# A two-layer hybrid mixer kernel: GLA's steps moved ahead to S5's input, and an LRU block's second gate moved one piece back

## The chip, the cores and the metric

One core of a Trainium2 chip runs the whole program in one launch. The metric is the device time of that execution in microseconds (us), lower is better; what is shown is the median of several runs. A profiled execution gives the rows that are read below.

## The reference

The input is one sequence of 512 tokens of width 1024, in float32. Two layers follow each other; each normalises the stream, projects it, runs four causal mixers beside each other, multiplies each by its SiLU path, merges the four with sigmoid gates and adds the result to the stream. A final RMSNorm ends it.

```python
for l in range(DEPTH):                       # DEPTH = 2
    u = rmsnorm(h, norm_gain[l])
    (gq, gk, gv, glr, gg, rq, rk, rv, rg, lx, lg, su, sg) = split_columns(u @ w_in[l])
    o_gla = gla_mix(gq, gk, gv, glr, ...) * silu(gg)        # chunked linear attention, 8 chunks of 64
    o_ret = retention_mix(rq, rk, rv, ...) * silu(rg)
    o_lru = rglru_mix(lx, ...) * silu(lg)                   # conv of 4, two sigmoid gates, linear scan
    y5 = gelu(s5_scan(su, ...)); y5 = y5 * sigmoid(y5 @ s5_glu_w[l] + s5_glu_b[l])
    o_s5 = y5 * silu(sg)
    merged = sum(sigmoid(u @ w_merge_gate[l, b]) * (o_b @ w_branch[l, b]) for the four b)
    h = h + merged @ w_out[l]
return rmsnorm(h, final_norm_gain)
```

In `rglru_mix` the two gates are `r = sigmoid(xb @ w_a + b_a)` and `i = sigmoid(xb @ w_x + b_x)`; with `a = exp(-8 r softplus(-lam))` the scan is `h_t = a h_(t-1) + xc i sqrt(1 - a^2)`.

## The kernel before

**Projections.** Almost all of TensorE's time goes to products with streamed weights. Each weight tile of 128x1024 comes by one DMA (`emit_raw`, L234), is copied by ACT as `hi` (L242), and DVE forms the rest `lo` (L243); a product is then three matmuls, `hi·uh`, `hi·ul`, `lo·uh` (L268 to L270 in `mm3`). A projection `proj_c` makes 128 channels for 512 tokens: 8 parts, 24 matmuls of 128x512. `PLAN` sets the order of the projections; weights are made some projections ahead with high priority.

**Pieces.** After every second part of `mm3`, that is after six matmuls, `bg.tick()` is called; such a stretch is called a *piece*, and a projection has four. `Bg` (L176 and on) holds generators for background work. Each has a time in ticks, and at every tick the first one in the list whose time has come runs one step, at most one step a tick (`PER_TICK = 1`). What a generator yields is the number of ticks until its next step. TensorE's own order is the order in which the code is written out, tick by tick; for the other engines the framework's scheduler sets the order ahead of time, from the same program, and each engine then runs its list in order.

**PSUM.** The main products have three buffers (`PM = 3`, tag `pm`), and the LRU gates take theirs from the same three. Five buffers (`ps`) serve the small matmuls.

**The stretch that the change touches** lies in each layer between GLA's projections and the first merge. Four projections make S5's input (`proj_c()` in L894 to L897: ACT copies each into `su`, tag `c4a`, and 32 small DMAs bring it to `uc`). Eight projections follow for the LRU: for m = 0 to 3 one `lx` and one `lg`. After them `merge(0)` begins with two gate projections. Beside these run two kinds of generators:

- `gla_core` (L852 on): the first step transposes the keys (L861). Then `attention` (L647 on) runs for t = -1 to 4, one *step* each: `values` (L691), the transposes of the last step's output (L713), `inter` (L702), `scores` (L658), `kv` (L672), on DVE the masks (L866) and the state updates (L682), then `norm`: squares on ACT (L871), a sum on DVE (L873), a power on POOL (L287), the product on DVE (L877). The next step's transposes read that product.
- `lru_block` m (L904 on), added when `lx` of m is done. Its first step makes the convolution: L915 on ACT and three L917 on DVE read the `lx` buffer and write `xc`, whose buffer `ac0` or `ac4` is shared by blocks m and m+2. It then yields 9 ticks. The second step is gate 0 (three matmuls, L924) and its Tanh on ACT (L929). The third is gate 1 (L924 again), the ACT operations L934, L935, L936, the DVE operations L937 to L943, POOL's L942 and L945, the square root on ACT (L944, which needs another activation table, so a table load stands before it and one after it), and the scan L946 and L947 on DVE. L947 is the last reader of `xc`.

```python
pa = gate(0); tr = s2()
act.activation(tr, pa, AF.Tanh, scale=0.5, bias=hc[:, 3, m:m + 1])     # L929
yield 1
px = gate(1)
act.activation(gl, px, AF.Tanh, ...)                                   # L934
act.activation(tl, tr, AF.Tanh, ...); act.activation(rl, tr, AF.Exp, ...)   # L935, L936
```

Gates of block m stand inside the projection `lg` of m+1 (block 3's inside the second gate projection of the merge).

Of the kernel before, what the change touches and what calls it, by code (L numbers as in the profile page):

```python
# [104 lines left out]
def hybrid_kernel(tc, x, wch, wgv, pcols, wlr, lrubd, s5a, s5bc, s5d, gains, ident_d, smask_d, rmask_d, rope_d,  # L105
# [19 lines left out]
    def big(tag, shape, dt=F32):  # L125
        return bp.tile(shape, dt, tag=tag, name=nm(tag))

    def s2(shape=(P, 512), dt=F32):
        return sm.tile(list(shape), dt, tag="s2", name=nm("s2"), bufs=S2B)

    def one(tag, shape, dt=F32, bufs=1):
        return sm.tile(list(shape), dt, tag=tag, name=nm(tag), bufs=bufs)

    def tiny(shape):
        return sm.tile(list(shape), F32, tag="tiny", name=nm("ty"), bufs=12)

    def psm(shape=(P, 512)):
        return pm.tile(list(shape), F32, tag="pm", name=nm("pm"))

    def pss(shape=(P, 512)):  # L140
        return pp.tile(list(shape), F32, tag="ps", name=nm("ps"))
# [79 lines left out]
    bg = Bg()  # L221
# [52 lines left out]
    def split(dst_h, dst_l, src, scale=None):  # L274
        if scale is None:
            act.activation(dst_h, src, AF.Copy)
            dve.tensor_tensor(dst_l, src, dst_h.bitcast(F32), SUB)
        else:
            act.activation(dst_h, src, AF.Copy, scale=scale)
            dve.scalar_tensor_tensor(dst_l, src, scale, dst_h.bitcast(F32), op0=MUL, op1=SUB)  # L280


    def rstd_of(ss, n, scale):
        ms = tiny([P, n])
        dve.tensor_scalar(ms, ss, scale, EPS, op0=MUL, op1=ADD)  # L285
        r = tiny([P, n])
        pool.tensor_tensor(r, ms, neghalf[:, :n], ALU.pow)  # L287
        return r
# [497 lines left out]
    for l in range(DEPTH):  # L786
# [4 lines left out]
        v = big("v8", [P, NT, W])  # L791
# [15 lines left out]
        dec = one("dec", [P, 2, 8])  # L807
# [44 lines left out]
        S = big("S4", [P, 4, 2, DV])  # L852

        def gla_core(E=E, kt_=kt_, v=v, sil=sil, oh=oh, ol=ol, S=S, dec=dec, hc=hc):
            kt = one("kt", [P, NT, 256])
            for t2 in range(2):
                pt = pss([P, 2, 2, P])
                for j in range(2):
                    for hp in range(2):
                        tt = 2 * t2 + j  # L860
                        pe.transpose(pt[:, j, hp], kt_[:, hp, tt * P:(tt + 1) * P], ident)  # L861
                act.activation(kt[:, 2 * t2:2 * t2 + 2], pt.rearrange("p j a b -> p j (a b)"), AF.Copy)
            yield 3

            def mask(dst, src, par, r):
                dve.copy_predicated(dst, smask[r, None, :].to_broadcast([64, 2, 64]), src)  # L866

            def norm(po):
                sq = s2([P, 2, 2, DV])
                for par in range(2):  # L870
                    act.activation(sq[:, par], po[par], AF.Square)  # L871
                ss = tiny([P, 2, 2])
                dve.tensor_reduce(ss, sq, axis=AX.X, op=ADD)  # L873
                r = rstd_of(ss.rearrange("p a b -> p (a b)"), HEADS, 1.0 / DV).rearrange("p (a b) -> p a b", a=2)
                on = s2([P, 2, 2, DV])
                for par in range(2):
                    dve.tensor_tensor(on[:, par], po[par], r[:, par, :, None].to_broadcast([P, 2, DV]), MUL)  # L877
                return lambda h: on[:, h % 2, h // 2]

            def final(t, pT):  # L880
                ts = slice(t * P, (t + 1) * P)
                p = s2([P, HEADS, P])
                for h in range(HEADS):
                    dve.scalar_tensor_tensor(p[:, h], pT[:, h], hc[:, 0, h:h + 1], sil[:, h, ts], op0=MUL, op1=MUL)
                split(oh[:, :, ts], ol[:, :, ts], p)

            yield from attention(lambda b, hp, cs: E[b:b + 64, 0, hp, cs], lambda b, hp, cs: E[b:b + 64, 1, hp, cs],
                                 kt, v, S, lambda hp, n: dec[:, hp, n:n + 1], mask, norm, final, 6)

        gg_ = bg.add(gla_core(), 3)  # L890


        uc = [big(f"uc{i}", [P, 8, P]) for i in range(2)]
# [12 lines left out]
        def lru_block(m, ps, of):  # L906
            t0 = 4 * (m % 2)
            wbd = one("wbd", [P, 2, P])
            sp.dma_start(wbd, lrubd[l, :, m::4])
            wbh, wbl = one("wbh", [P, 2, P], F32R), one("wbl", [P, 2, P], F32R)  # L910
            split(wbh, wbl, wbd)
            xc = big(f"ac{t0}", [P, T])
            xh, xl = (big(f"ac{t0 + i}", [P, T], F32R) for i in (1, 2))
            cw = lambda j: pc[:, PC["cw"][0] + 4 * m + j:PC["cw"][0] + 4 * m + j + 1]
            act.activation(xc, ps, AF.Identity, scale=cw(3), bias=col("cb", m))  # L915
            for s in (1, 2, 3):
                dve.scalar_tensor_tensor(xc[:, s:], ps[:, :T - s], cw(3 - s), xc[:, s:], op0=MUL, op1=ADD)  # L917
            split(xh, xl, xc)
            yield 9

            def gate(i):
                g = psm()
                for n, (a, b) in enumerate(((wbh, xh), (wbh, xl), (wbl, xh))):
                    pe.matmul(g, a[:, i], b, start=n == 0, stop=n == 2)  # L924
                return g

            pa = gate(0)
            tr = s2()
            act.activation(tr, pa, AF.Tanh, scale=0.5, bias=hc[:, 3, m:m + 1])  # L929
            yield 1  # L930
            px = gate(1)
            gl = big(f"ac{t0 + 3}", [P, T])
            tl, rl = (big(f"ac{t0 + i}", [P, T]) for i in (1, 2))
            act.activation(gl, px, AF.Tanh, scale=0.5, bias=hc[:, 4, m:m + 1])  # L934
            act.activation(tl, tr, AF.Tanh, scale=spl[:, 0, m:m + 1], bias=spl[:, 0, m:m + 1])  # L935
            act.activation(rl, tr, AF.Exp, scale=spl[:, 2, m:m + 1], bias=spl[:, 2, m:m + 1])  # L936
            dve.tensor_scalar(rl, rl, 0.5, 0.5, op0=MUL, op1=ADD)  # L937
            q = s2()
            dve.scalar_tensor_tensor(q, tl, 1.0, rl, op0=ADD, op1=MUL)
            dve.scalar_tensor_tensor(rl, q, -2.0, rl, op0=ADD, op1=MUL)  # L940
            dve.scalar_tensor_tensor(gl, gl, 1.0, xc, op0=ADD, op1=MUL)
            pool.tensor_tensor(gl, gl, rl, MUL)  # L942
            dve.scalar_tensor_tensor(rl, tl, -1.0, rl, op0=ADD, op1=MUL)  # L943
            act.activation(tl, tl, AF.Sqrt)  # L944
            pool.tensor_tensor(gl, gl, tl, MUL)  # L945
            dve.tensor_tensor_scan(xc, rl, gl, 0.0, MUL, SUB)  # L946
            dve.scalar_tensor_tensor(of[:, m], xc, 0.5, of[:, m], op0=MUL, op1=MUL)  # L947

        lbs = []
        for m in range(4):  # L950
            ps = proj_c()
            if m >= 2:
                bg.finish(lbs[m - 2])
            lbs.append(bg.add(lru_block(m, ps, ofl)))
            silu2(ofl[:, m], proj_c())
# [293 lines left out]
```

## Time and profile before

| | |
|---|---|
| median of 3 runs | 1257.12 us (1256.19 to 1259.31) |
| the profiled execution | 1255.62 us |
| its span, first to last instruction | 1253.8 us |
| mean granted clock of TensorE | 0.996 of full speed |
| busy: PE, DVE, ACT, POOL | 1212.6, 809.8, 529.6, 508.4 us |
| PE in the 40 slices of the span | 9 tenths or more in 38, 5 in the first, 7 in the last |

A slice is 31 us. All rows of the trace are from that one profiled execution, so that sums are made against its 1255.62 us. A row of the timeline has the start, the duration, engine, line, operation, result and operands, and in brackets the idle time of the engine before it with what ended it. The duration of a matmul is modelled to its end in PSUM and is longer than its share of the engine: while TensorE is not held up, one 128x512 matmul starts about 0.23 us after the other.

### The profile page before, as it was taken

The page shows a single profiled execution, that of the slowest core. Times are in us where ns is not written, and L with a number is a line of the kernel's source. Part 1 is how long each engine was busy: PE and PEld are TensorE (multiplying, and loading weights), DVE is VectorE, ACT ScalarE, POOL GpSimd, SP SyncE. Part 2 cuts the span into 40 slices and gives each one's busy share as a digit, 9 for nine tenths or more (in the row PEclk, how much of TensorE's full clock was granted, in tenths as well). Part 3 has the DMA queues.
Part 4 walks back from the last instruction along what each step waited for, and adds up shares of the span by engine and source line. Part 5 has one row for each costly group of instructions (what it writes and reads, how often), then busy time and mean ns, then how long its engine had stood idle before and what let it go on. Part 6 is the DMA issues. An engine that isn't in the chain of part 4 may idle for free. (4 is left out here: it accounts for less than half of the span.)

```text
span 1253.8 us, 17315 instructions
## 1 busy us (share of the span) xinstructions
PE 1212.6 (97%) x6444; PEld 1008.0 (80%) x6444; DVE 809.8 (65%) x1411; ACT 529.6 (42%) x824; POOL 508.4 (41%) x588
## 2 busy tenths in 40 slices
PE   5999999989999999999999999999899999999997
PEld 5888868877888888888898887788778888888886
DVE  6974875477599896744354467746756988446433
ACT  5622475434434622532355235744345354333322
POOL 8780313578666568000201012238887563000001
PEclk9999999999999999999999999999999999999999
DMA  6233323213322423433342232232222234333322
GB/s 227 85 106 106 102 76 106 93 38 105 96 77 83 135 87 98 137 99 101 103 135 101 84 112 83 84 105 76 72 89 84 66 101 137 96 123 101 90 79 84
DMA packets 49796, 124.25 MB, mean 99 GB/s; under 512 B 8272, under 2 KB 21040, under 8 KB 49712
## 3 DMA queue, kind: packets, MB, share of 16 engines
q1 hardware_dynamic: 49712, 123.15, 31.2%
q8 instruction: 51, 0.84, 0.3%
q14 instruction: 33, 0.27, 0.1%
HBM read 114.73 MB, written 4.19 MB: 95 GB/s over the span
## 5 line engine op out<-in xcount | busy, mean ns | idle before, releaser
L243 DVE TENSOR_TENSOR lo<-raw,hi 128x1024 fp32r<-128x1024 f32 (+1 forms) x196 | 262.0, 1340 | 214.6 <-ACT hi L242 212.0
L268 PE MATMUL pm<-uh,hi 128*128 128x512 f32 x960 | 378.3, 394 | 5.0 <-ACT ac L934 3.3
L242 ACT ACTIVATE hi<-raw 128x1024 fp32r<-128x1024 f32 (+1 forms) x196 | 207.8, 1061 | 415.1 <-PE pm L269 284.6
L270 PE MATMUL pm<-uh,lo 128*128 128x512 f32 x960 | 374.4, 390 | 0.0
L269 PE MATMUL pm<-ul,hi 128*128 128x512 f32 x960 | 374.3, 390 | 0.0
L268 PEld LDWEIGHTS pm<-uh,hi 128*128 128x128 f32 x960 | 180.3, 188 | 48.7 <-ACT ac L934 5.0
L270 PEld LDWEIGHTS pm<-uh,lo 128*128 128x128 f32 x960 | 180.3, 188 | 37.9
L269 PEld LDWEIGHTS pm<-ul,hi 128*128 128x128 f32 x960 | 180.4, 188 | 36.2
L268 PE MATMUL pm<-oh,hi 128*128 128x512 f32 x256 | 101.0, 395 | 0.0
L270 PE MATMUL pm<-oh,lo 128*128 128x512 f32 x256 | 99.8, 390 | 0.0
L269 PE MATMUL pm<-ol,hi 128*128 128x512 f32 x256 | 99.8, 390 | 0.0
L1135 POOL TENSOR_TENSOR ac<-c4a,S 128x512 f32<-128x512 f32 x2 | 2.6, 1294 | 239.5 <-DVE c4a L1133 239.5
L287 POOL TENSOR_TENSOR ty<-ty,c 128x4 f32<-128x4 f32 x16 | 16.9, 1057 | 118.8 <-DVE ty L285 118.1
L358 PE MATMUL pm<-hi,uh 128*128 128x512 f32 x128 | 52.6, 411 | 5.1 <-ACT v L1028 3.8
L268 PEld LDWEIGHTS pm<-oh,hi 128*128 128x128 f32 x256 | 48.1, 188 | 11.3 <-issue 1.7
L270 PEld LDWEIGHTS pm<-oh,lo 128*128 128x128 f32 x256 | 48.1, 188 | 10.1
L269 PEld LDWEIGHTS pm<-ol,hi 128*128 128x128 f32 x256 | 48.1, 188 | 9.6
L360 PE MATMUL pm<-lo,uh 128*128 128x512 f32 x128 | 50.9, 398 | 0.0
L359 PE MATMUL pm<-hi,ul 128*128 128x512 f32 x128 | 50.9, 398 | 0.0
L531 POOL TENSOR_TENSOR c<-x,x 128x128 f32<-128x128 f32 x32 | 16.1, 522 | 67.3 <-PE ps L559 67.2
L599 DVE TENSOR_TENSOR_SCAN gt<-s5f,r 128x128 f32<-128x128 f32 x64 | 41.7, 710 | 0.3
L606 POOL TENSOR_TENSOR sw<-sw,sin 128x512 f32<-128x512 f32 x16 | 27.2, 1697 | 36.3 <-ACT sw L603 36.3
(320 smaller groups left out, 2187.2 us busy)
## 6 DMA issues: line engine op xcount, KB each, us to landing
raw<-in_wch SPq DMA_DIRECT2D x192, 512.0 KB, 3.5
raw<-in_wgv SPq DMA_DIRECT2D x4, 544.0 KB, 4.8
uc<-in_x SPq DMA_DIRECT2D x4, 512.0 KB, 6.4
bc<-in_s5bc SPq DMA_DIRECT2D x16, 128.0 KB, 2.1
uc<-c4a SPq DMA_DIRECT2D x64, 32.0 KB, 2.0
v<-uc SPq DMA_DIRECT2D x128, 16.0 KB, 2.3
out<-ac SPq DMA_DIRECT2D x8, 256.0 KB, 2.1
S<-in_gains SPq DMA_DIRECT2D x3, 512.0 KB, 5.1
```

The costliest lines, as they stand in the source:

```text
L242: act.activation(hi, raw, AF.Copy)
L243: dve.tensor_tensor(lo, raw, hi.bitcast(F32), SUB)
L268: pe.matmul(ps, lh, rh, start=i == 0, stop=False)
L269: pe.matmul(ps, lh, rl, start=False, stop=False)
L270: pe.matmul(ps, ll, rh, start=False, stop=i == n - 1)
L287: pool.tensor_tensor(r, ms, neghalf[:, :n], ALU.pow)
L358: pe.matmul(ps[tt], xh(k, ts), wh, start=k == 0, stop=False)
L359: pe.matmul(ps[tt], xl(k, ts), wh, start=False, stop=False)
L360: pe.matmul(ps[tt], xh(k, ts), wl, start=False, stop=k == KD - 1)
L531: pool.tensor_tensor(vz[:, :, :, gg], x1[:, gg::2], x2[:, gg::2], ADD)
L599: dve.tensor_tensor_scan(gt[:, g], par["f"][:, 3, g0 + g:g0 + g + 1].to_broadcast([P, P]), r1[:, g], 0.0, MUL, ADD)
L606: pool.tensor_tensor(sw, sw, sin, MUL)
```

## The change

Three numbers of the GLA generator change, and one of the LRU block. The GLA core starts at the first tick of S5's input, not at the third; its first attention step comes two ticks after the transposes, not three; and its steps are four ticks apart, not six. An LRU block's gate 1 comes two ticks after gate 0, not one. No operation is added or removed.

```diff
@@ gla_core
                 act.activation(kt[:, 2 * t2:2 * t2 + 2], pt.rearrange("p j a b -> p j (a b)"), AF.Copy)
-            yield 3
+            yield 2
...
-                                 kt, v, S, lambda hp, n: dec[:, hp, n:n + 1], mask, norm, final, 6)
-
-        gg_ = bg.add(gla_core(), 3)
+                                 kt, v, S, lambda hp, n: dec[:, hp, n:n + 1], mask, norm, final, 4)
+
+        gg_ = bg.add(gla_core(), 1)
@@ lru_block
             act.activation(tr, pa, AF.Tanh, scale=0.5, bias=hc[:, 3, m:m + 1])
-            yield 1
+            yield 2
             px = gate(1)
```

What that does to the order is shown at three places of layer 0; layer 1 has the same. The number behind a name is that of the buffer's use, and `waits` names the engine whose semaphore the instruction waits for.

The first place is TensorE at the start of S5's input (`pm_1035` is its first projection), as a difference, with the key transposes L861, and the first scores L658 and state products L672 of the GLA core.

```order
 L269 MATMUL pm_1035<-ul_113,hi_959 128x512
 L270 MATMUL pm_1035<-uh_112,lo_960 128x512
-L861 MATMUL ps_1055<-c_114,c4b_615 128x128 x4
-L861 MATMUL ps_1061<-c_114,c4b_615 128x128 x4
+L658 MATMUL ps_1067<-e_104_613 64x64 x2
+L658 MATMUL ps_1068<-e_104_613 64x64 x2
+L658 MATMUL ps_1067<-e_104_613 64x64 x2
+L658 MATMUL ps_1068<-e_104_613 64x64 x2
+L672 MATMUL ps_1067<-v_84_431,kt_1042 64x128 x4
 L268 MATMUL pm_1035<-uh_112,hi_959 128x512
 L269 MATMUL pm_1035<-ul_113,hi_959 128x512
```

Where the transposes stood, after three pieces, the first attention step stands now; the transposes stand after the first piece. The later steps come after three pieces of a projection each, 24 matmuls apart: t = 0, 1 and 2 in the second, third and fourth projection of S5's input, t = 3 and 4 in `lx` and `lg` of m = 0. Before, t = 0 stood behind the third of them and t = 4 ahead of `lg` of m = 2.

The second place is TensorE at gate 1 of block 1 (`pm_1713`, now `pm_1719`), which stands in `lg` of m = 2 (`pm_1673`) ahead of `lx` of m = 3 (`pm_1749`). Before:

```order
L924 MATMUL pm_1713<-ac_244_1530,wbh_1525 128x512 [waits Activation_49]
L924 MATMUL pm_1713<-ac_245_1531,wbh_1525 128x512
L924 MATMUL pm_1713<-ac_244_1530,wbl_1526 128x512
L268 MATMUL pm_1673<-uh_112,hi_1512 128x512
L269 MATMUL pm_1673<-ul_113,hi_1512 128x512
L270 MATMUL pm_1673<-uh_112,lo_1513 128x512
L268 MATMUL pm_1673<-uh_112,hi_1512 128x512
L269 MATMUL pm_1673<-ul_113,hi_1512 128x512
L270 MATMUL pm_1673<-uh_112,lo_1513 128x512
L268 MATMUL pm_1749<-uh_112,hi_1626 128x512 [waits Activation_49]
```

Now:

```order
L269 MATMUL pm_1673<-ul_113,hi_1562 128x512
L270 MATMUL pm_1673<-uh_112,lo_1563 128x512
L924 MATMUL pm_1719<-ac_255_1580,wbh_1575 128x512 [waits Activation_49]
L924 MATMUL pm_1719<-ac_256_1581,wbh_1575 128x512
L924 MATMUL pm_1719<-ac_255_1580,wbl_1576 128x512
L268 MATMUL pm_1749<-uh_112,hi_1638 128x512 [waits Activation_49]
```

The piece that stood between gate 1 and the next projection now stands before gate 1; both still wait for ACT. The same holds for block 2 and the first merge gate (`pm_1856`).

The third place is ACT's list from gate 0 of block 1 (its Tanh, L929) to L935. L915 is the convolution of block 2 and waits for DVE; L242 makes a weight's `hi`; L276 splits the next gates' weights; L934 empties gate 1. Before:

```order
L929 ACTIVATE s_280_1705<-pm_1701,hc_213 128x512 [waits Activation_49]
L276 ACTIVATE wbh_1682<-wbd_1680 128x256 [waits DMAHW1_49,PE_49]
L936 ACTIVATE ac_284_1719<-s_280_1705,spl_248 128x512 [waits Activation_49]
L934 ACTIVATE ac_282_1717<-pm_1713,hc_213 128x512 [waits PE_49]
L935 ACTIVATE ac_283_1718<-s_280_1705,spl_248 128x512
L915 ACTIVATE ac_276_1686<-pm_1630,pc_211 128x512 [waits DVE_49]
L242 ACTIVATE hi_1776<-raw_1774 128x1024 [waits DMAHW0_49,PE_49]
```

Now:

```order
L929 ACTIVATE s_280_1705<-pm_1701,hc_213 128x512 [waits PE_49]
L915 ACTIVATE ac_276_1686<-pm_1642,pc_211 128x512 [waits DVE_49]
L242 ACTIVATE hi_1776<-raw_1774 128x1024 [waits DMAHW0_49,PE_49]
L276 ACTIVATE wbh_1682<-wbd_1680 128x256 [waits DMAHW1_49,PE_49]
L936 ACTIVATE ac_284_1725<-s_280_1705,spl_248 128x512 [waits Activation_49]
L934 ACTIVATE ac_282_1723<-pm_1719,hc_213 128x512 [waits PE_49]
L935 ACTIVATE ac_283_1724<-s_280_1705,spl_248 128x512
```

L915 and L242 have moved ahead of the three operations that follow gate 1. At block 2 the list before already had L915 (of block 3) ahead of them, followed by L276, L936 and L934; there only L242 is new between them. From the S5 scan on, TensorE's order is the same as before.

## Rows read from the trace of the kernel before

**Rows 1.** The page, part 1: busy time, share of the span, instructions of each engine.

```profile
PE 1212.6 (97%) x6444; PEld 1008.0 (80%) x6444; DVE 809.8 (65%) x1411; ACT 529.6 (42%) x824; POOL 508.4 (41%) x588
```

**Rows 2.** Waits of PE, whole span: line, releaser, us in total, times, longest.

```profile
PE ps L1023 <- DVE s L1016: 6.4, 2, 3.2
PE pm L358 <- ACT v L1028: 3.8, 2, 1.9
PE pm L268 <- ACT ac L934: 3.3, 4, 1.5
PE pm L924 <- ACT s L929: 2.7, 4, 1.2
PE pm L268 <- ACT s L929: 1.6, 2, 0.8
```

**Rows 3.** Timeline of PE, layer 0, from the end of `lx` of m = 3.

```profile
169.82 0.39 PE L270 MATMUL pm<-uh,lo 128*128 128x512 f32 x1
170.23 0.50 PE L268 MATMUL pm<-uh,hi 128*128 128x512 f32 x1
...
177.54 0.39 PE L270 MATMUL pm<-uh,lo 128*128 128x512 f32 x1
179.41 0.50 PE L268 MATMUL pm<-uh,hi 128*128 128x512 f32 x1 [1.48 <-ACT ac L934]
179.75 0.39 PE L269 MATMUL pm<-ul,hi 128*128 128x512 f32 x1
...
187.73 0.62 PE L924 MATMUL pm<-ac,wbh 128*128 128x512 f32 x2
...
188.42 0.40 PE L268 MATMUL pm<-uh,hi 128*128 128x512 f32 x1
```

**Rows 4.** Timeline of ACT, POOL and DVE, layer 0, from that end to L934.

```profile
170.02 1.06 ACT L242 ACTIVATE hi<-raw 128x1024 fp32r<-128x1024 f32 x1 [2.83 <-PE pm L269]
...
170.98 0.62 ACT L276 ACTIVATE ac<-ac 128x512 fp32r<-128x512 f32 x1
...
171.62 1.28 ACT L944 ACT_TABLE_LOAD   x1
...
172.91 0.63 ACT L944 ACTIVATE ac<-ac 128x512 f32<-128x512 f32 x1
...
173.68 1.30 POOL L945 TENSOR_TENSOR ac<-ac,ac 128x512 f32<-128x512 f32 x1 [5.18 <-ACT ac L944]
...
175.01 1.23 DVE L946 TENSOR_TENSOR_SCAN ac<-ac,ac 128x512 f32<-128x512 f32 x1 [1.84 <-POOL ac L945]
...
176.27 0.69 DVE L947 SCALAR_TENSOR_TENSOR of<-ac,of 128x512 f32<-128x512 f32 x1
...
177.00 0.78 ACT L915 ACTIVATE ac<-pm,pc 128x512 f32<-128x512 f32 x1 [1.46 <-DVE of L947]
...
177.68 0.41 ACT L276 ACTIVATE wbh<-wbd 128x256 fp32r<-128x256 f32 x1
...
177.99 0.80 ACT L936 ACTIVATE ac<-s,spl 128x512 f32<-128x512 f32 x1
...
178.69 0.67 ACT L934 ACTIVATE ac<-pm,hc 128x512 f32<-128x512 f32 x1
```

**Rows 5.** Timeline of DVE, layer 0, block 2 ahead of its square root.

```profile
185.87 0.69 DVE L943 SCALAR_TENSOR_TENSOR ac<-ac,ac 128x512 f32<-128x512 f32 x1 [1.18 <-POOL ac L942]
```

**Rows 6.** Timeline of PE and DVE, layer 0, GLA's step t = 2.

```profile
131.68 1.05 PE L691 MATMUL ps<-v,c 128*128 128x128 f32 x8
...
134.36 0.50 PE L268 MATMUL pm<-uh,hi 128*128 128x512 f32 x1
...
138.37 0.75 DVE L877 TENSOR_TENSOR s<-ps,ty 128x256 f32<-128x256 f32 x2
```

**Rows 7.** Windows: stretch, its length, busy PE, PEld, DVE, ACT, POOL (x), PEclk, DMA share, GB/s.

```profile
274.00:277.30 3.30, 0.11 (x2) 0.03 (x1) 3.30 (x4) 0.13 (x1) 3.30 (x4) 1.00 0.00 0
278.00:281.40 3.40, 3.40 (x12) 2.74 (x10) 3.40 (x3) 0.56 (x1) 1.94 (x2) 0.50 0.00 0
```

## The prediction

> **What bounds the kernel now.** I read the busy times first. TensorE (PE) is busy for 1212.6 of 1253.8 us [rows 1], so the work of the other engines costs time only where PE waits for it. The waits of PE come second [rows 2]. Two kinds belong to the stretch that the change touches: waits for the Tanh of gate 0 (L929), 2.7 and 1.6 us, and waits for the Tanh of gate 1 (L934), 3.3 us. That is 7.6 us in ten waits, five a layer. The S5 input beside them has no row there: GLA holds up nobody today. Third is PE's timeline. A listed wait costs more than its idle time: from 177.54 to 179.41 are 1.87 us where 0.23 is usual, and the matmul behind takes 0.34 in place of 0.23 to be followed, so the listed 1.48 costs 1.75 us [rows 3], 0.27 more. Ten waits then cost 7.6 + 2.7 = 10.3 us. One short hold in each layer is not listed (169.82 to 170.23, 0.18 + 0.11 us [rows 3]); with both, the LRU stretch loses 10.9 us. No change there can win more.
>
> Fourth is what stands behind the longest of these waits, and this decides the forecast. Call E the end of `lx` of m = 3, 169.82 + 0.23 = 170.05. From E the next projection but one, the merge's first, started at 179.41, E + 9.36 [rows 3]. PE's own work in between is 24 matmuls of `lg` and two gates. From 179.41 to 187.73 are 36 matmuls and one restart of 0.11, so 0.228 us each; a gate is 188.42 - 187.73 = 0.69 [rows 3]. That makes 24 x 0.228 + 1.38 = 6.85 us. The other 2.5 us are waits, and the chain that makes them runs over four engines [rows 4]: L242, which waited 2.83 us for PE to end `lx`; L276; the table load; the square root L944; POOL's L945; the scan L946; L947; then L915 of block 3, which had waited 1.46 us for L947 because it writes the buffer that L947 reads; then L276, L936 and L934, which empties gate 1. L934 needs nothing of L915. It is behind it in ACT's list, and an engine runs its list in order: gate 1 was through PE before 177.0, L934 ran at 178.69.
>
> **The change, term by term.**
>
> *GLA's steps, two ticks earlier and four apart.* The same instructions are issued, at other places. Its cover is the distance between steps. Step t = 2 began at 131.68, PE was back at the projection at 134.36, and the product that the next transposes read was ready at 138.37 + 0.75 = 139.12, 7.4 us after the beginning [rows 6]. Now the next transposes come after 2.68 us of the step, 24 matmuls (5.5 us) and the next `values` (0.9 us), 9.1 us after the beginning: 1.7 us to spare. From t = 3 to t = 4 scores, products and `values` fall away, and the spare shrinks to nearly nothing. I take 0 here; the ends are 0 and 0.5 us a step. The key transposes come one piece (6 x 0.228 = 1.37 us) after the key projection, and two DVE products like L947 (0.69 each [rows 4]) lie between: 1.38 us and a semaphore. I take 0.1 us a layer, 0.2 in all. The DMAs of S5's input and the weights move against each other in SP's list. Weights are made projections ahead: L242 waits for PE, not for its DMA [rows 4], so I cost that at nothing. ACT's third copy of S5's input waits for those DMAs, and behind it stand the squares of step t = 2; the spare 1.7 us covers them, and what came later than that would be added to PE.
>
> *Gate 1 one piece later: what goes.* Gate 1 now comes two pieces (2.7 us) after gate 0, and L929 takes 0.7. The six waits for L929 go: 2.7 + 1.6 us [rows 2] and 6 x 0.27, in all 5.9 us. At `lx` of m = 2 nothing takes their place: block 0's gates have no scan in front of them.
>
> *Gate 1 one piece later: what comes.* PE's work between E and the next projection but one stays 6.85 us; the piece has only changed sides. So that start is set by the chain, if the chain is longer. For block 2 (from `lx` of m = 3 to the merge) it is the chain of rows 4 with two edits: L276 at 170.98 (0.64 to its follower) is no longer in front of the table load, and an L242 (0.96 to its follower, 170.02 to 170.98) now stands between L915 and L934. E + 9.36 - 0.64 + 0.96 = E + 9.68. The wait costs 9.68 - 6.85 + 0.11 = 2.9 us.
>
> For block 1 (from `lx` of m = 2 to `lx` of m = 3) the change is larger. Before, L934 stood ahead of L915; now L915 and an L242 are ahead of it, so the same chain of 9.68 us holds there too. One piece of it is longer: the table load waits for DVE's L943, which waits for POOL's L942 [rows 5], and gate 1 of block 0 is a piece later. From the end of that gate I count about 2.0 us of ACT until L934 is through, four DVE operations like L947 (2.6 us when queued), L942 as long as L945 (1.3 us [rows 4]) and L943 (0.7), in sum about 6.7; `lx` takes 5.5 of them, so L943 ends near E + 1.3, where the load could have begun at E + 0.93 (170.98 [rows 4]). I add 0.4: the wait costs 3.3 us. Its bounds are 2.9 (nothing late) and 3.8.
>
> *The sum of waits.* Per layer 2.9 + 3.3 = 6.2 us, for both layers 12.5, in place of 10.9: +1.6, and with GLA's 0.2 **+1.8 us**. Five waits a layer become two long ones.
>
> *TensorE's clock.* The two waits of 3.2 us for L1016 [rows 2] were the longest of the kernel in full run. The first is the stretch 274.0 to 277.3, and soon behind it PE was granted 0.50, that is 1.2 in place of 2.4 GHz, from 278.0 to 281.4 [rows 7]. At half speed 3.4 us cost 1.7. The two waits of 1.9 us (L1028) [rows 2] show no such stretch. The new waits have idle times of about 3.1 (block 1) and 2.7 us (block 2), between these. The bounds are no stretch and four, 0 and 6.8 us. Going by the nearest row I take one behind the longer wait of each layer: **+3.4 us**. [...]
>
> The sum is 1.8 + 3.4 = +5.2 us on the profiled 1255.62: **1260.8 us**. The median of the runs shown, 1257.12, is 1.5 above that execution; on it the same sum would be 1262.3.
>
> **The rivals.**
>
> 1. *The long waits without the clock.* If PE keeps its clock behind waits of 2.7 to 3.1 us, 1255.62 + 1.8 = 1257.4. For it: the 1.9 us waits were not followed. Against it: 3.2 us were, twice. Chance 0.33.
> 2. *All four waits are followed by a half-speed stretch:* 1255.62 + 1.8 + 6.8 = 1264.2. Chance 0.09.
> 3. *Faster: L915 is not late.* GLA's work on DVE and ACT leaves the LRU stretch. If that ends the scan of block m early enough, L915 passes at once and L934 runs right behind gate 1. Then four waits of about 0.67 (L934 [rows 4]) plus 0.4 are left, 4.3 in place of 10.9: 1255.62 - 6.6 + 0.2 = 1249.2. It decides at L947: it must end by about E + 3, not E + 6.3 as in rows 4. For it: part of the queue was GLA's. Against it: L242 waits for PE at E, and from there the load, L944, L945, L946 and L947 have no GLA work among them. Chance 0.11.
> 4. *GLA's steps are too close.* If PE waits 0.5 us for the product L877 at each of five steps, 5.0 us come on top of rival 1: 1262.4. Rows 6 speak against it except at the last step. Chance 0.05.
>
> **How the numbers follow.** The forecast has 0.42. A measurement of this kernel can tell about 0.3% from no change, here 3.8 us. Slower by more than that are the forecast for the most part (0.35), rival 2 (0.09), rival 4 (0.04) and a little of rival 1 (0.02): 0.50. Within it are the rest of the forecast (0.07), rival 1 (0.31) and the rest of rival 4: 0.39. Faster is rival 3: 0.11. The range goes from rival 1 with the block-1 waits at 2.9 and block 2's somewhat shorter (1255.5) to rival 2 with the median's 1.5 us on top (1266.0); it leaves out rival 3 and the tails. The forecast's own range is 1258.5 to 1263.
>
> **What would show it.** In the profile after, PE's waits for L929 should be gone, and those for L934 should be four, two of about 3.1 and two of about 2.7 us, at the first matmul of `lx` of m = 3 and of the merge, 9.7 to 10.1 us after the `lx` before. L915 should be waiting for L947 right before each. The windows behind should show a granted clock of 0.50 for 3.4 us, once a layer. No wait of PE for L877, L866 or L682 should appear. It is wrong if L934 runs at once behind gate 1, if the waits at the merge are under 1.5 us, or if PE waits in S5's input.

## The result and the profile after

| | before | after |
|---|---|---|
| median | 1257.51 us (1256.19 to 1259.31, 4 runs) | 1266.45 us (1264.31 to 1267.98, 4 runs) |
| ratio | | 1.0075, 95% interval 1.0062 to 1.0087 |
| the profiled execution | 1255.62 us | 1266.81 us |
| its span | 1253.8 us | 1265.0 us |
| mean granted clock | 0.996 | 0.990 |

The change made the kernel slower by 8.9 us, or 0.75%. Slower was forecast, but at 1260.8, and 1266.45 lies 0.45 above the range.

The busy times of the changed kernel, as in [rows 1]:

```profile
PE 1219.5 (96%) x6444; PEld 1014.4 (80%) x6444; DVE 810.6 (64%) x1411; ACT 530.1 (42%) x824; POOL 505.9 (40%) x588
```

PE has as many instructions as before and is busy for 6.9 us more; that is a first hint at its clock, since nothing was added. The waits of PE, as in [rows 2] (line, releaser, us in total, times, longest):

```profile
PE pm L268 <- ACT ac L934: 11.7, 4, 3.1
PE ps L314 <- ACT ac L304: 10.5, 2, 9.2
PE ps L1023 <- DVE s L1016: 6.4, 2, 3.2
PE pm L358 <- ACT v L1028: 3.8, 2, 1.9
```

No row names L929 any more, and L934 has four waits of 11.7 us in place of four of 3.3. L1016 and L1028 read as before. L304 is the start of the program (9.6 us before); the change does not touch it. PE has no wait at all from 100 to 140 us, where the moved GLA steps now stand.

The four waits on PE's timeline, layer 0, which answers to [rows 3]: the first row is the last matmul of `lx` of m = 2, then come the end of gate 1 of block 1 and `lx` of m = 3 behind it, and at last the end of `lx` of m = 3, the end of gate 1 of block 2 and the merge.

```profile
155.28 0.39 PE L270 MATMUL pm<-uh,lo 128*128 128x512 f32 x1
...
162.13 0.40 PE L924 MATMUL pm<-ac,wbl 128*128 128x512 f32 x1
165.63 0.50 PE L268 MATMUL pm<-uh,hi 128*128 128x512 f32 x1 [3.10 <-ACT ac L934]
165.97 0.39 PE L269 MATMUL pm<-ul,hi 128*128 128x512 f32 x1
...
167.16 0.63 PE L268 MATMUL pm<-uh,hi 128*128 128x512 f32 x1
167.59 0.63 PE L269 MATMUL pm<-ul,hi 128*128 128x512 f32 x1
168.01 0.63 PE L270 MATMUL pm<-uh,lo 128*128 128x512 f32 x1
...
172.60 0.39 PE L270 MATMUL pm<-uh,lo 128*128 128x512 f32 x1
...
179.45 0.40 PE L924 MATMUL pm<-ac,wbl 128*128 128x512 f32 x1
182.62 0.50 PE L268 MATMUL pm<-uh,hi 128*128 128x512 f32 x1 [2.77 <-ACT ac L934]
```

The reader sees two things. The idle times are 3.10 and 2.77 us, and the starts lie 10.1 us (165.63 - 155.51) and 9.8 us (182.62 - 172.83) behind the end of the `lx` before, which is the start of its last matmul plus 0.23. And 1.5 us behind a wait the distance from one matmul to the next goes from 0.23 to 0.43 us.

The windows of the changed kernel show that this is the clock. They are all the stretches ahead of the program's last few us in which the profile shows a clock of 0.50 (columns as in [rows 7]), each 3.4 us long. The first, second, fourth and fifth go with the four waits for L934, the third and the sixth with L1016 as before, and the last follows the wait for L1028 in layer 1:

```profile
167.10:170.50 3.40, 3.40 (x9) 2.63 (x8) 2.98 (x5) 0.88 (x2) 0.34 (x1) 0.50 0.50 176
184.10:187.50 3.40, 3.40 (x10) 2.61 (x9) 2.97 (x5) 0.86 (x2) 0.35 (x1) 0.51 0.52 182
283.10:286.50 3.40, 3.40 (x12) 2.71 (x11) 3.40 (x3) 0.28 (x1) 1.65 (x2) 0.50 0.00 0
784.90:788.30 3.40, 3.40 (x9) 2.65 (x9) 3.40 (x7) 1.48 (x3) 0.00 (x0) 0.50 0.69 194
801.90:805.30 3.40, 3.40 (x10) 2.62 (x9) 3.40 (x7) 1.45 (x3) 0.00 (x0) 0.51 0.47 154
900.90:904.30 3.40, 3.21 (x10) 2.73 (x11) 3.40 (x4) 0.60 (x1) 2.84 (x3) 0.51 0.00 0
924.80:928.20 3.40, 3.40 (x12) 2.71 (x11) 3.17 (x3) 1.80 (x3) 3.40 (x4) 0.51 0.00 0
```

That is seven stretches where the kernel before had two, both behind L1016. The bill of the two profiled spans: five more stretches by 1.7 us are 8.5; the waits cost 11.7 + 4 x 0.27 = 12.8 in place of 10.9, so 1.9 more; the start-up wait is 0.9 longer. The sum is 11.3, and the spans differ by 11.2 us. Executions of one kernel do not all have the same number of stretches (the fastest kernel below, profiled twice, had one and three), so the medians, 8.9 apart, need not show quite as many. All four runs of the changed kernel have a mean clock of 0.988 to 0.990, so the profiled one is no exception.

What makes the waits stands on ACT's timeline of the changed kernel, which answers to [rows 4]:

```profile
156.90 1.28 ACT L944 ACT_TABLE_LOAD   x1 [0.36 <-DVE ac L943]
...
162.28 0.78 ACT L915 ACTIVATE ac<-pm,pc 128x512 f32<-128x512 f32 x1 [1.45 <-DVE of L947]
162.95 1.04 ACT L242 ACTIVATE hi<-raw 128x1024 fp32r<-128x1024 f32 x1
163.90 0.40 ACT L276 ACTIVATE wbh<-wbd 128x256 fp32r<-128x256 f32 x1
164.20 0.80 ACT L936 ACTIVATE ac<-s,spl 128x512 f32<-128x512 f32 x1
164.91 0.67 ACT L934 ACTIVATE ac<-pm,hc 128x512 f32<-128x512 f32 x1
```

L915, which had waited 1.45 us for L947, starts at 162.28. Gate 1 ends on PE at 162.53 (162.13 + 0.40), but L242, L276 and L936 still pass before L934, which empties it. At block 2 the same list runs from 179.25 to the start of L934 at 181.89.

### The profile page after: what moved, and what is told of

Read it like the earlier page. It is cut to its first block, busy times and chain, and to the rows that moved or that the text cites. A ratio compares the mean times of both kernels' runs of the same rounds, so it can differ in the third digit from the quotient of the medians.

```text
span 1265.0 us, 17310 instructions
## 1 busy us (share of the span) xinstructions
PE 1219.5 (96%) x6444; PEld 1014.4 (80%) x6444; DVE 810.6 (64%) x1411; ACT 530.1 (42%) x824; POOL 505.9 (40%) x588
## 5 line engine op out<-in xcount | busy, mean ns | idle before, releaser
L268 PE MATMUL pm<-uh,hi 128*128 128x512 f32 x960 | 380.0, 396 | 12.0 <-ACT ac L934 11.7
L242 ACT ACTIVATE hi<-raw 128x1024 fp32r<-128x1024 f32 (+1 forms) x196 | 207.8, 1061 | 412.0 <-PE pm L269 285.0
L268 PEld LDWEIGHTS pm<-oh,hi 128*128 128x128 f32 x256 | 48.0, 188 | 11.3 <-issue 1.7
L942 POOL TENSOR_TENSOR ac<-ac,ac 128x512 f32<-128x512 f32 x8 | 10.3, 1292 | 93.6 <-DVE ac L940 93.6
L531 POOL TENSOR_TENSOR c<-x,x 128x128 f32<-128x128 f32 x32 | 16.8, 544 | 66.4 <-PE ps L559 66.3
```

The costliest lines, as they stand in the source:

```text
L242: act.activation(hi, raw, AF.Copy)
L268: pe.matmul(ps, lh, rh, start=i == 0, stop=False)
L531: pool.tensor_tensor(vz[:, :, :, gg], x1[:, gg::2], x2[:, gg::2], ADD)
```

## The experiments

Two things had to be told apart: what makes the waits, and what makes the rest of the loss. Theory A says that the GLA moves cost nothing and that the late convolution (L915, held by the shared buffer `xc`) makes the long waits; theory C says that most of the loss is TensorE's clock behind these waits. (The text of the second run below gives the letter C to another thought, that the gates alone are the whole loss.) Each kernel was timed in five rounds, beside the kernel before on the same chip, and has an interval.

**The GLA moves alone.** The changed kernel, but with the gates one piece apart.

```diff
             act.activation(tr, pa, AF.Tanh, scale=0.5, bias=hc[:, 3, m:m + 1])
-            yield 2
+            yield 1
```

> Only the GLA steps are moved; the gates stay one piece apart. Theory A (the long waits come from gate 1 being one piece later, with L915 ahead of L934 in ACT's list): no wait of PE for L934 above 2 us, no stretch at half clock in the LRU part, so no slower than before; waits in the LRU part about 4 to 5 us per layer's two in place of 5.5, time 1253 to 1257.5. Theory B (the GLA steps, closer together, are what costs): slower, 1262 to 1266, with PE waiting in S5's input or with the long waits for L934 still there.

Measured: 1254.88 us beside 1257.46, ratio 0.9982 [0.9972, 0.9992]. Alone they make the kernel 2.6 us faster. The waits of PE for the two Tanh:

```profile
PE pm L268 <- ACT ac L934: 5.9, 4, 1.5
...
PE pm L924 <- ACT s L929: 0.3, 1, 0.3
```

Ten waits of 7.6 us became five of 6.2: 1.4 less idle time and five restarts of 0.27 less are 2.75 us. No wait of PE stands in S5's input here either. So GLA's moves alone are no loss.

**The gates alone.** The kernel before with the yield of 2 between the gates.

```diff
             act.activation(tr, pa, AF.Tanh, scale=0.5, bias=hc[:, 3, m:m + 1])
-            yield 1
+            yield 2
```

> Only gate 1 is one piece later; GLA's steps stay where they were. In ACT's list L934 of block 1 now stands ahead of L915, that of block 2 behind it. Theory A: one long wait per layer, at the merge, 2.7 us idle, and about 1 us or less at lx of m = 3; a half-clock stretch behind the long one if the clock falls there; 1255 to 1259. Theory B (GLA's steps are the cost): all of the loss is gone and the gates' waits with it, 1251 to 1253. Theory C (the gates alone are the whole loss): 1264 to 1267.

Measured: 1264.37 us, ratio 1.0062 [1.0046, 1.0077]: 6.9 of the 8.9 us come with the gates alone, and theory A's 1255 to 1259 missed. The merge's wait is the long one (2.76 us in layer 0), that of `lx` of m = 3 is 1.55 with one of 0.74 for L929 just ahead of it. Both were followed in layer 0. The rows are the waits on PE's timeline, then a window behind each:

```profile
162.49 0.74 PE L924 MATMUL pm<-ac,wbh 128*128 128x512 f32 x2 [0.74 <-ACT s L929]
...
165.01 0.59 PE L268 MATMUL pm<-uh,hi 128*128 128x512 f32 x1 [1.55 <-ACT ac L934]
...
182.01 0.53 PE L268 MATMUL pm<-uh,hi 128*128 128x512 f32 x1 [2.76 <-ACT ac L934]
```

```profile
166.00:169.00 3.00, 3.00 (x9) 2.33 (x8) 3.00 (x6) 0.82 (x2) 0.00 (x0) 0.55 0.63 213
182.50:186.00 3.50, 3.50 (x11) 2.72 (x10) 3.50 (x8) 1.28 (x3) 0.00 (x0) 0.53 0.64 190
```

So a wait need not be near 3 us to be followed. It need not be followed either: the same wait in layer 1, 1.57 us, was not. The two waits of 1.9 us for L1028 both were, so that this trace too has seven stretches.

At `lx` of m = 3 L934 runs ahead of L915 here (164.29 and 164.86 on ACT's timeline). It is GLA's moves on top of the gates' that put L915 in front of it there, and 0.74 and 1.55 us become the 3.10 us of the changed kernel. So the two parts of the change do not add up: with the gates moved, GLA's moves give nothing back (1266.45 with them, 1264.37 without, intervals that overlap).

**The convolution's own buffer.** The changed kernel, but the convolution no longer writes the buffer that the scan of the block before still reads.

```diff
-            xc = big(f"ac{t0}", [P, T])
+            xc = big(("c4b", "ac4", "ac0", "c4b")[m], [P, T])
```

> As changed, but the LRU blocks' convolution results rotate over three buffers (the GLA key buffer, idle by then, is the third), so that L915 of block m+2 doesn't wait for the scan of block m. Theory A: the four long waits for L934 vanish (each under 1 us), the half-clock stretches in the LRU part with them, and the waits for L929 stay away: 1246 to 1251, faster than both kernels. Theory D (L934 is late for another reason, as the order of the list itself or the table loads): waits of 2 us or more stay, 1258 or more.

Measured: 1249.63 us, ratio 0.9943 [0.9928, 0.9958]: 16.8 us below the changed kernel, and faster than the kernel before. Run once more beside the last experiment below, it gave 1251.54, 0.9956 [0.9944, 0.9969].

> The changed kernel with the convolution's own buffer, run again to stand beside the next one: 1248.5 to 1251 us by its first run (1249.63).

The second run lies 0.5 us above what was expected of it; the two intervals overlap. No wait for L934 is left, but the waits for L929 did not stay away as expected: each trace has two of 1.2 us. From PE's waits and ACT's timeline of the first run:

```profile
PE pm L924 <- ACT s L929: 2.3, 2, 1.2
```

```profile
156.24 0.76 ACT L915 ACTIVATE ac<-pm,pc 128x512 f32<-128x512 f32 x1
157.02 1.28 ACT L944 ACT_TABLE_LOAD   x1
...
164.86 0.67 ACT L934 ACTIVATE ac<-pm,hc 128x512 f32<-128x512 f32 x1
```

L915 now runs 6 us earlier, ahead of the table load. Yet L934 runs at 164.86, as late as in the changed kernel (164.91), since now L276, which waits 1.42 us for DVE's L917, stands ahead of it. But nobody waits for it: gate 1's last matmul starts at 161.93 on PE, and the next projection at 162.32. What the early convolution gives PE is another accumulator. By the program's allocation, `lx` of m = 3 takes the one that `lx` of m = 2 had, which L915 and L917 have read by then; in the changed kernel it is given gate 1's, and so it must wait for the Tanh that empties it. The late L934 costs only where the next projection needs its buffer. So theory A holds in that the waits go with the convolution's buffer, but the link is the accumulator and not an earlier L934. No run changes the buffer and leaves the accumulators as they were.

**The buffer on the other orders.** The same line on the kernel before, and on the GLA moves alone.

> The kernel before with one edit: the convolution of block m writes a buffer that the block before does not read to its end. Theory A (L915's wait for the scan's last product is what makes the waits for L934): the four waits for L934 (3.3 us listed, 4.4 with the restarts) go, the waits for L929 stay (4.3 us listed): 1252 to 1255 us. Rival (the gain of the same edit on the changed kernel came from the gates two pieces apart with it, L915's place in ACT's list matters only there): within 0.1% of before, 1256 to 1259 us.

> GLA's moves and the convolution's own buffer, gate 1 left one piece behind gate 0. Theory A: from the kernel with GLA's moves alone (1254.9) the four waits for L934 (5.9 us listed) go, those for L929 (0.3 us) come back to at most 2: 1248.5 to 1251 us, about the same as with the gates two pieces apart (1249.6). Rival (two pieces between the gates are worth something of their own once L915 is out of the way): 1252 to 1255 us.

Measured: 1253.23 us, 0.9967 [0.9954, 0.9980], and 1252.46, 0.9958 [0.9946, 0.9970]. No wait for L934 is left in either. The intervals overlap with those of the two runs of the last kernel (0.9943 and 0.9956): with its own buffer the convolution makes the kernel 4 to 8 us faster than before in any of the three orders. The first is as theory A has it. The second one missed its band by 1.5 us: L929's waits came back to 3.2 us, and two of 0.4 for L917 are new. Between gates one and two pieces apart these runs can't decide.

**Filling the waits.** The changed kernel with 18 transposes behind gate 1 of blocks 1 and 2, whose output nothing reads (2.0 us of PE).

```diff
             px = gate(1)
+            if m in (1, 2):
+                pz = pss()
+                for i in range(18):
+                    pe.transpose(pz[:, i % 4 * P:(i % 4 + 1) * P], ident, ident)
```

> As changed, with 18 transposes of the identity into an unread small PSUM tile behind gate 1 of blocks 1 and 2, about 2.0 us of PE work inside each long wait. Theory A with the clock as part of the loss: the starts behind the waits stay where the chain sets them, the idle time falls to about 1.1 and 0.7 us, PE keeps its clock, and 4 times 1.7 us come back: 1258.5 to 1261. If the half-clock stretches don't come from PE's idling: 1265 to 1268, with stretches at 0.50 still behind these places.

Measured: 1257.22 us, ratio 0.9999 [0.9991, 1.0008]: 9.2 us back by added work, a little more than expected. The waits and the stretches behind them, layer 0:

```profile
162.10:165.60 3.50, 2.37 (x20) 2.02 (x19) 2.62 (x4) 3.36 (x6) 0.00 (x0) 1.00 0.00 0
165.70:169.10 3.40, 3.40 (x15) 2.80 (x16) 3.40 (x8) 1.67 (x3) 0.00 (x0) 1.00 0.59 190
177.80:181.00 3.20, 2.39 (x21) 2.03 (x19) 2.52 (x3) 3.20 (x6) 0.00 (x0) 1.00 0.00 0
181.10:184.50 3.40, 3.40 (x15) 2.81 (x16) 3.40 (x8) 1.67 (x3) 0.00 (x0) 1.00 0.54 189
```

The projection starts at 165.60 as in the changed kernel (165.63), since the chain on ACT sets that; only what PE does until then is different, and behind it 15 matmuls start in 3.4 us in place of 9. This is the clock's part by itself, and it is theory C's. Matched by the starts of the same matmuls, the two traces show 1.6 us won at each of the four places, 6.4 in all, about what four stretches cost. The other 2.4 of the 8.8 us between the two profiled spans lie where nothing was filled: no stretch follows L1028 here (1.6 less), 1.7 us less are lost around the end of the first layer, and the two stretches at L1016 last 6.8 us in place of 3.4 (1.0 more).

**Filling one place only, and half.** Block 1 only; then 9 transposes at both.

> The changed kernel with the 18 transposes behind gate 1 of block 1 only; the waits at the merge stay near 2.8 us. Theory C (each long wait pays its own half-clock stretch, 1.7 us): half of the 9.2 us that the filler at both places gave back, 1261 to 1263 us, with a stretch behind each merge wait and none behind the filled ones. Rival (the first long wait of a layer makes the second one's stretch, as by a phase that it shifts): the stretches go at both places, 1257 to 1259 us, or stay at both, 1265 to 1267 us.

> The changed kernel with 9 transposes in place of 18 behind gate 1 of blocks 1 and 2: 1.0 us of the four long waits is filled, idle times of about 2.0 us are left. Theory C1 (a wait of this length is mostly not followed by a half-clock stretch, as most of the waits of 1.5 us and those of 1.9 us in the kernel before): 1257 to 1260 us, waits for the gate's Tanh 7.5 to 8.5 us in all, at most one stretch in four places. Rival C2 (any wait of over 1.5 us in these places is followed): 1264 to 1267 us, with a stretch behind three or four of the four.

Measured: 1261.74 us, 1.0040 [1.0028, 1.0051], and 1261.30, 1.0030 [1.0020, 1.0040]. The first is as theory C has it: no stretch behind the filled waits, one behind each merge wait. With half of the filler neither reading held: the wait at `lx` of m = 3, 2.12 us idle, was not followed, that at the merge, 1.79 idle, was, in both layers. The two waits of layer 0 on PE's timeline (L938 is L934 four lines on) and a window behind each, from the half filler's trace:

```profile
164.98 0.50 PE L268 MATMUL pm<-uh,hi 128*128 128x512 f32 x1 [2.12 <-ACT ac L938]
...
180.39 0.50 PE L268 MATMUL pm<-uh,hi 128*128 128x512 f32 x1 [1.79 <-ACT ac L938]
```

```profile
165.10:168.50 3.40, 3.40 (x15) 2.78 (x16) 3.40 (x8) 1.66 (x3) 0.00 (x0) 1.00 0.67 187
...
181.80:185.20 3.40, 3.40 (x10) 2.69 (x9) 3.04 (x6) 0.94 (x2) 0.28 (x1) 0.54 0.51 182
```

The longer idle time kept the clock and the shorter lost it, so the length alone does not decide. What does, these runs leave open.

**The same filler, late.** The 18 transposes come one piece later, inside the projection that has waited.

```diff
             dve.scalar_tensor_tensor(of[:, m], xc, 0.5, of[:, m], op0=MUL, op1=MUL)
+            if m in (1, 2):
+                yield 1
+                pz = pss()
+                for i in range(18):
+                    pe.transpose(pz[:, i % 4 * P:(i % 4 + 1) * P], ident, ident)
```

> The changed kernel with the same 18 transposes per place, but one piece later: behind the first six matmuls of the projection that waited, so that they fill nothing. Theory C (the filler helps because PE has work inside the wait): the four waits stay at 2.7 to 3.1 us, three or four of them are followed by a half-clock stretch, and the transposes add their own 2.0 us at each place, 8 in all: 1272 to 1278 us. Rival (the extra instructions help in another way, by the order that they give the other engines, or they cost nothing anywhere): waits shorter or stretches gone, 1257 to 1267 us.

Measured: 1267.56 us, ratio 1.0086 [1.0073, 1.0099], below the band, because only half of what it rests on came about. At `lx` of m = 3 the wait and the half clock stayed, and the transposes themselves ran at half speed (PE's timeline):

```profile
165.37 0.50 PE L268 MATMUL pm<-uh,hi 128*128 128x512 f32 x1 [3.09 <-ACT ac L934]
...
166.86 3.79 PE L952 MATMUL ps<-c 128*128 128x128 f32 x18
170.41 0.48 PE L268 MATMUL pm<-uh,hi 128*128 128x512 f32 x1
...
182.08 0.48 PE L268 MATMUL pm<-uh,hi 128*128 128x512 f32 x1 [0.45 <-DVE ac L917]
...
183.54 2.13 PE L952 MATMUL ps<-c 128*128 128x128 f32 x18
185.43 0.48 PE L268 MATMUL pm<-uh,hi 128*128 128x512 f32 x1
```

The 18 took 3.55 us there (166.86 to 170.41) and 1.89 at the merge (183.54 to 185.43). At the merge the wait shrank to 0.45 and is one for L917, not L934: with this order the merge has been given another accumulator there too, and L934 ran at 182.71, behind the merge's start. The convolution has no buffer of its own here, so this shows the link by the accumulator once more: L934 is late, and the merge does not wait for it. So fillers of 2 x 5.4 = 10.9 us came, and two waits (some 5.3) and two stretches (3.4) went: +2.2, and the medians differ by 1.1. That is no full account, since other waits moved as well (two of 1.3 us at L713 are new). For the merge the kernel is no control; at `lx` it is one: there, in both layers, work outside the wait did not keep the clock.

**Filling another wait.** The version with the own buffer, and 24 transposes in the 3.2 us waits for L1016.

```diff
                 yield 8
+                if tt == 0:
+                    pz = pss()
+                    for i in range(24):
+                        pe.transpose(pz[:, i % 4 * P:(i % 4 + 1) * P], ident, ident)
                 pt = pss([P, 4, P])
```

> The same kernel with 24 unread transposes in the 3.2 us waits for L1016 too, one in each layer, which leaves about 0.5 us of each. Theory C: the half-clock stretches behind these waits go, one or two of 1.7 us each, and the filler costs next to nothing since it lies inside the wait: 1246 to 1248.5 us. Rival (after L1016 it is something else that lowers the clock, or the transposes delay the pieces behind them): 1249 to 1252 us.

Measured: 1251.38 us, 0.9964 [0.9951, 0.9978], beside 1251.54 without the filler: nothing gained. The stretch behind L1016 is gone, as theory C has it (the window from 274.5 to 278.0 us, where the first run of the version without the filler lost its clock), but the waits that follow have grown. The window, and PE's waits:

```profile
274.50:278.00 3.50, 3.50 (x20) 2.73 (x19) 3.50 (x3) 0.60 (x1) 2.46 (x2) 1.00 0.00 0
```

```profile
PE pm L358 <- ACT v L1032: 5.5, 2, 2.8
PE pm L358 <- DVE s L1003: 4.2, 4, 1.6
PE ps L1027 <- DVE s L1016: 1.4, 2, 0.7
```

L1032 is L1028 four lines on. In the trace that the version without the filler left beside it they were 3.8 and 1.4 us. PE came sooner to waits whose end other engines set, and 1.7 + 2.8 = 4.5 us of new idle time took what the clock gave.

## Why the prediction was off

1. **GLA at nothing: right.** No wait came in S5's input. The moves alone gain 2.6 us: the waits for L929 shrink from 4.3 to 0.3 us, most likely since GLA's work no longer stands beside the gates on DVE and ACT. In the whole change that gain is gone, since the gates' move removes these waits anyway; there the moves lengthen the wait at `lx` of m = 3, which the forecast had in the gates' term.
2. **The six waits for L929 go: right.** None is left.
3. **The chain from E: right.** Forecast were starts at E + 10.1 and E + 9.7 us and idle times of 3.1 and 2.7; measured 10.1 and 9.8, 3.10 and 2.77. The table load waits 0.36 us for L943 (0.4 taken). The sum of the waits is 12.8 against 12.5, so +1.9 in place of +1.6. Left out was a link: L934 costs PE time because the next projection has gate 1's accumulator; where it had another, an equally late L934 cost nothing.
4. **The clock: wrong, and this is the step that failed.** "Going by the nearest row I take one behind the longer wait of each layer: +3.4 us." All four waits were followed, so what stands behind them was 6.8 us and not 3.4; filling them gave 6.4 back at these places. In layer 1 the 1.9 us wait for L1028 was followed as well, +1.7, which the forecast took as safe since neither of the two was followed before. That this fifth stretch comes from the change is not shown: behind L1028 it comes and goes from trace to trace. With 8.5 the sum is 1255.62 + 1.8 + 8.5 = 1265.9, and the start-up wait, 0.9 longer, makes up the rest to the 1266.81 of the profiled execution.
5. **The chances.** Rival 2, four stretches, had 0.09; it is what happened, and its 1264.2 lacks the fifth stretch and the start-up's 0.9 us. (With the median's 1.5 us on top it is 1265.7, not the 1266.0 that the range ends at.) The Trainium skill, in TensorE: Matmul & The Clock Gate, section "HAM oscillation — how this bites in real kernels", tells of a kernel whose every group of matmuls stood behind a DMA wait of about 3 to 5 us and started at half speed. The trace agrees for the four waits here, of 2.76 to 3.10 us. Other traces of this case have shorter waits that were followed (1.55 us in the gates alone, 1.79 with half of the filler), and waits that were not: 2.12 us with half of the filler, and 3.20 us for L1016 in layer 1 of the first run with the own buffer (one stretch in that trace, in layer 0). So four out of four could not be told from the rows before; one per layer was a choice between the bounds, and it was the wrong one.

Rival 3, L915 not late, was put at 1249.2 us. The own buffer makes its condition true and measures 1249.63 and 1251.54. That the numbers are near is partly luck: L934 does not run right behind gate 1, as the rival had it; the next projection no longer needs it.

## What to carry to other kernels

When several short waits of TensorE are to be merged into fewer long ones, price the half-speed stretch behind every one of them, not only behind the longest: here 1.9 us more of waits brought 6.8 us of lost clock behind them. Ask then which buffer PE waits for, and what holds it: a convolution held by a shared SBUF buffer kept its accumulator, so that the next projection was given the one that a late Tanh empties. One line that gives the convolution a buffer of its own turned a loss of 0.75% into a gain of about 0.5%. Where PE soon comes to a wait that other engines end, speed won ahead of it can come back as idle time there, as in the last experiment.

## What had not been expected of the hardware

- Adding 2.0 us of transposes that nobody reads to each of four waits made the kernel 9.2 us faster (1266.45 to 1257.22), 6.4 of them at these places.
- Idle time alone does not tell whether the clock falls: 1.79 us was followed by a stretch at 0.50 and 2.12 was not, in one trace; 3.2 us (L1016) was not followed in layer 1 of two traces, while 1.55 us was in another; nor were the waits of 2.8 us in the trace of the last experiment, which has no such stretch ahead of its last few us.
- A stretch at 0.50 lasted 3.4 us each time in the changed kernel, whatever the wait before it (1.92 to 3.2 us). In other traces it sometimes lasted 6.8, as behind L1016 in the kernel with the filled waits.
